# FFN in-projections as seven Strassen block products, the running sum z in DRAM, one new SBUF layout

## The chip, the cores and the metric

The kernel runs on one core of a Trainium2 chip. TensorE (PE) multiplies, VectorE (DVE), ScalarE (ACT) and GpSimd (POOL) do the elementwise work, SyncE (SP) issues most of the loads. The metric is the device time of one execution in microseconds, the median of several runs.

## The reference, cut to what matters

Two layers act on 512 latent and 256 context tokens of width 1024. Each layer is: half-step SwiGLU FFN, token mixer (chunked gMLP in layer 0, grouped-query attention in layer 1), half-step FFN; each sub-layer is modulated and closed by a LayerNorm of `ALPHA * x + sublayer`.

```python
def swiglu(h, w_in, w_out):
    g, u = jnp.split(h @ w_in, 2, axis=-1)          # w_in: 1024 x 2*2816
    return (jax.nn.silu(g) * u) @ w_out             # w_out: 2816 x 1024

def ffn_sublayer(x, shift, scale, gate, w_in, w_out, ln_g, ln_b):
    y = swiglu(modulate(x, shift, scale), w_in, w_out)
    return layer_norm(ALPHA * x + 0.5 * gate * y, ln_g, ln_b)
```

Three of the four FFNs see all 768 tokens (`plan` in `body`: layer 0 first and second FFN, layer 1 first FFN), the last one only the 512 latents. All matrix products are taken in three float32r passes (`split` makes `hi + lo`; the products are hi·hi, hi·lo and lo·hi).

## The kernel before, in words

The 2816 columns of g and of u are cut into 22 tiles of 128. For one tile, `in_proj` runs over 8 slices of K = 1024 and three passes with the weights stationary: 48 matmuls with 512 latent columns for g and u, then 48 with 256 context columns. ACT and DVE then make `silu(g) * u` and split it (`glu`, in `ffn`). After a chunk of 3 or 4 tiles (`FFN_CHUNKS`) `out_proj` multiplies it back: per block of 128 tokens and half of D, `accumulate` runs 3 matmuls of 512 columns for each tile of the chunk, DVE multiplies PSUM by the gate (L421) and adds the result to `z`, which stays in SBUF (L422).

Weights come through `load_raw` (SP, 512 KB each) and `pump`: ACT copies the high part of a 128x1024 tile (L134), DVE subtracts for the low part (L135). Six such tiles are in flight (`W_BUFS`).

Behind this run the fillers. `mod_unit` works out one modulation vector on DVE by 8 steps of two slices of `w_mod` (L247: one operation for each slice and condition), and reduces it over the partitions on POOL (L255); `affine` turns z into `ALPHA * (zhat * g + b)` on DVE (L395). `fill` issues one step; `FFN_FILLS` and `MOD_PLAN` say where.

The last chunk of a sub-layer is closed by `End.inner`: while the next block is on PE, a block's LayerNorm is taken, z is normalised in place, transposed on PE, and becomes h^T of the next sub-layer. `opening` runs the first two tiles of the next FFN on the latents while h^T of the context (blocks 4 and 5, `make_h`) is still being made.

PE and the start keep the order of the program (`Pinned`). The order on the other queues is fixed when the program is compiled, by a scheduler that takes ready instructions in program order; a tile is given out again once its last reader is done. All helpers' instructions are recorded under the helper's line (all matmuls: L67; all splits: L134 and L135).

Of the kernel before, what the change touches and what calls it, by code (L numbers as in the profile page):

```python
# [7 lines left out]
F32 = mybir.dt.float32  # L8
# [34 lines left out]
FFN_FILLS = [(4, 3), (4, 4), (0, 8), (0, 0)]  # L43
# [13 lines left out]
class Pinned:  # L57
    """An engine whose instructions keep the order of the program."""
# [13 lines left out]
class Backbone:  # L72
# [32 lines left out]
    def banks(self, paired):  # L105
        if paired and self.pairs:
            ps = self.pair()
            return [ps[:, 0:512], ps[:, 512:1024]]
        return [self.bank(), self.bank()]

    def t3(self, *shape):
        return self.main.tile([P, *shape], F32, tag="t3", bufs=5, name="t3")

    def mid(self, *shape):
        return self.main.tile([P, *shape], F32R, tag="mid", bufs=4, name="mid")

    def sm(self, shape, name, bufs=4, dt=F32):
        if shape == [P]:
            name, bufs = "s512", 6
# [4 lines left out]
    # ------------------------------------------------------------ primitives  # L124
    def mm(self, out, lhsT, rhs, start, stop):
        self.pe.matmul(out, lhsT, rhs, start=start, stop=stop)
# [5 lines left out]
    def split(self, hi, lo, src):  # L132
        """src = hi + lo, each of them exact in float32r"""
# [14 lines left out]
    # -------------------------------------------------------------- weights  # L148
    def weight_order(self):
        io = self.io  # L150
        seq = []

        def ffn(l, s):
            wi = io["ffn_w_in"][l, s].rearrange("(k p) f -> p k f", p=P)
            wo = io["ffn_w_out"][l, s]
            f0 = 0
            for n in FFN_CHUNKS:
                for f in range(f0, f0 + n):
                    for o in (0, D_FF):
                        seq.append(wi[:, :, o + f * P : o + f * P + P])  # L160
                for f in range(f0, f0 + n):
                    seq.append(wo[f * P : f * P + P, :])
                f0 += n

        ffn(0, 0)
        wi = io["gmlp_w_in"][0].rearrange("(k p) f -> p k f", p=P)
        for cc in range(GMLP_HALF // 512):
            for q in range(4):
                o = GMLP_HALF + cc * 512
                seq.append(wi[:, 2 * q : 2 * q + 2, o : o + 512])  # L170
        seq.append(wi[:, :, 0:P])
        j0 = 0
        for n in GMLP_CHUNKS:
            for j in range(j0 + 1, min(j0 + n + 1, GMLP_CH)):
                seq.append(wi[:, :, j * P : j * P + P])
            for j in range(j0, j0 + n):
                seq.append(io["gmlp_w_out"][0][j * P : j * P + P, :])
# [3 lines left out]
        wq = io["attn_w_qkv"][0].rearrange("(k p) f -> p k f", p=P)  # L181
        for o in (1024, 0, 512):
            for q in range(4):
                seq.append(wq[:, 2 * q : 2 * q + 2, o : o + 512])
        for h in range(N_HEADS):
            seq.append(io["attn_w_o"][0][h * P : h * P + P, :])
        ffn(1, 1)
        self.wseq, self.wraw, self.wready, self.wlive, self.reserve = seq, [], [], 0, 0

    def load_raw(self, most=RAW_BUFS):  # L190
        while len(self.wraw) < most and self.wseq:
            src = self.wseq.pop(0)
            raw = self.main.tile([P, 1024], F32, tag="raw", bufs=RAW_BUFS, name="raw")
            dst = raw if len(src.shape) == 2 else raw[:, :].rearrange("p (a b) -> p a b", b=src.shape[2])
            self.sp.dma_start(dst, src)
            self.wraw.append(raw)

    def pump(self, most=9):
        """split as many of the coming weights as there is room for"""
        self.load_raw()  # L200
        while self.wlive + self.reserve < W_BUFS and self.wraw and most:
            raw = self.wraw.pop(0)
            w = self.main.tile([P, 2, 1024], F32R, tag="w", bufs=W_BUFS, name="w")
            for c in self.cuts:
                self.split(w[:, 0, c], w[:, 1, c], raw[:, c])
            self.wready.append(w)
            self.wlive += 1
            self.load_raw()
# [12 lines left out]
    # ----------------------------------------------------------- modulation  # L221
    def mod_raw(self):
        """the next slice of w_mod: 128 rows by 512 columns"""
        while len(self.mraw) < MRAW_BUFS and self.mseq:
            l, i, half, k = self.mseq.pop(0)
            o = i * D + half * 512
# [1131 lines left out]
```

## Time and profile before

| | |
|---|---|
| median of 3 runs | 2980.02 us (2976.21 to 2981.7) |
| span of the profiled execution, first to last instruction | 2969.7 us |
| median less span | 10.3 us |
| busy in that span: PE, DVE, ACT, POOL | 2912.1, 1967.8, 928.6, 285.3 us |
| moved by DMA | 296.63 MB, mean 100 GB/s |

The page gives no total of the profiled execution beside its span; 10.3 us is what lies around it if it ran like the median. Groups of instructions are named by line, engine, operation, and out<-in by the program's names, with count, busy time and mean length. In a timeline a row begins with start and length in us, and may merge several instructions (x2).

### The profile page before, as it was taken

Reading aid. Unit: us, or ns where it says so; the run is one execution under the profiler, and the core shown is the slowest. Engines: PE = TensorE matmul, PEld = TensorE weight load, DVE = VectorE, ACT = ScalarE, POOL = GpSimd, SP = SyncE. Lnnn points to the kernel's source line nnn. Section 1 sums busy time; section 2 is a strip of 40 time slices with the busy share of each in tenths; the row PEclk is TensorE's granted clock in tenths of the full one; section 3 lists DMA queues with packets and bytes.
Section 4 is the critical chain, followed back from the end, with each engine's and each line's share of the span. In section 5 each row is a group of like instructions: output and inputs, shape, how many; then the busy total and the mean of one; then the engine's idle time right before and its main releaser. Section 6 shows DMA issues by size and latency. Waiting matters only on the chain.

```text
span 2969.7 us, 38390 instructions
## 1 busy us (share of the span) xinstructions
PE 2912.1 (98%) x15241; PEld 2493.9 (84%) x15241; DVE 1967.8 (66%) x3259; ACT 928.6 (31%) x1603; POOL 285.3 (10%) x180
## 2 busy tenths in 40 slices
PE   7999999999999999999999999999999989999998
PEld 5888888888888888878888888888888878888886
DVE  7867756574377778896866649854433687874455
ACT  6121221432342433512121134111122547722222
POOL 0201110011100000010111102000000022010001
PEclk9999999999999999999999999999999999999999
DMA  8434433144322322243333213532222140153232
GB/s 261 129 93 122 134 92 95 43 149 152 125 84 72 102 76 79 63 137 100 121 107 112 88 57 114 168 95 64 62 66 71 43 125 21 60 163 101 86 94 69
DMA packets 311178, 296.63 MB, mean 100 GB/s; under 512 B 12040, under 2 KB 248632, under 8 KB 311000
## 3 DMA queue, kind: packets, MB, share of 16 engines
q1 hardware_dynamic: 308120, 284.76, 31.8%
q0 software_dynamic: 2880, 9.44, 0.8%
q8 instruction: 119, 1.95, 0.3%
q14 instruction: 59, 0.48, 0.0%
HBM read 282.62 MB, written 11.53 MB: 99 GB/s over the span
## 4 chain that ended last, share of the span: by engine, by line
PE 85%; DVE 8%; ACT 2%; DMA 2%; issue 1%; POOL 1%; SPq 0%; DVEq 0%; POOLq 0%; ACTq 0%
PE ps L67 85%; DVE z L395 2%; DVE acc L247 2%; DVE w L135 1%; DMA mod_raw<-in_w_mod_dram 1%; PE pp L67 1%; DMA mraw<-in_w_mod_dram 0%; DVE z L67 0%; DVE mid L135 0%; POOL rs L145 0%; ACT t L867 0%; ACT t L865 0%; DVE t L538 0%; DVE t L421 0%; ACT pT L134 0%
## 5 line engine op out<-in xcount | busy, mean ns | idle before, releaser
L67 PE MATMUL ps<-hA,w 128*128 128x512 f32 (+1 forms) x4896 | 1110.1, 386 | 1.1 <-DVE w L135 0.9
L67 PEld LDWEIGHTS ps<-hA,w 128*128 128x128 f32 x4896 | 900.7, 188 | 180.8 <-DVE w L135 1.3
L67 PE MATMUL ps<-w,mid 128*128 128x512 f32 x3768 | 871.0, 391 | 8.6 <-ACT mid L134 5.2
L67 PEld LDWEIGHTS ps<-w,mid 128*128 128x128 f32 x3768 | 706.4, 189 | 157.9 <-ACT mid L134 6.8
L134 ACT CAST w<-raw 128x1024 fp32r<-128x1024 f32 (+1 forms) x363 | 368.7, 1032 | 894.1 <-issue 416.8
L135 DVE TENSOR_TENSOR w<-raw,w 128x1024 fp32r<-128x1024 f32 (+1 forms) x363 | 456.5, 1261 | 262.5 <-ACT w L134 261.8
L67 PEld LDWEIGHTS ps<-hB,w 128*128 128x128 f32 x3744 | 461.1, 192 | 8.8 <-DVE hB L135 1.0
L67 PE MATMUL ps<-hB,w 128*128 128x256 f32 x3744 | 464.2, 283 | 1.3 <-ACT hB L134 0.7
L421 DVE SCALAR_TENSOR_TENSOR t<-ps,gate 128x512 f32<-128x512 f32 x368 | 252.4, 689 | 196.0 <-PE ps L67 193.4
L538 DVE TENSOR_TENSOR t<-t,ps 128x512 f32<-128x512 f32 (+1 forms) x154 | 87.8, 571 | 349.2 <-PE ps L67 306.6
L134 ACT CAST mid<-t 128x512 fp32r<-128x512 f32 (+2 forms) x226 | 122.1, 556 | 553.3 <-DVE t L538 389.4
L247 DVE SCALAR_TENSOR_TENSOR acc<-mraw,cs,acc 128x512 f32<-128x512 f32 x392 | 277.8, 746 | 11.9 <-DMA mraw<-in_w_mod_dram 11.5
L422 DVE TENSOR_TENSOR z<-z,t 128x512 f32<-128x512 f32 x368 | 263.6, 723 | 8.7
L255 POOL PARTITION_ALL_REDUCE t<-acc x36 | 125.2, 3519 | 859.2 <-DVE z L422 570.7
L67 PE MATMUL ps<-w,hA 128*128 128x512 f32 x816 | 190.6, 390 | 0.0
L537 ACT ACTIVATE t<-ps 128x512 f32<-128x512 f32 (+1 forms) x154 | 77.9, 506 | 355.9 <-PE ps L67 324.8
L67 PEld LDWEIGHTS ps<-w,hA 128*128 128x128 f32 x816 | 153.3, 188 | 31.9
L145 POOL TENSOR_TENSOR rs<-ve,mhalf 128x1 f32<-128x1 f32 (+3 forms) x47 | 35.4, 756 | 1413.5 <-DVE ve L142 1057.5
L135 DVE TENSOR_TENSOR mid<-t,mid 128x512 fp32r<-128x512 f32 (+2 forms) x226 | 141.1, 637 | 44.9 <-ACT mid L134 44.7
L255 POOL PARTITION_ALL_REDUCE gate<-acc x20 | 75.2, 3791 | 247.9 <-DVE acc L247 240.5
L67 PE MATMUL ps<-w,hB 128*128 128x512 f32 x336 | 82.6, 397 | 2.8 <-ACT hB L360 2.1
L395 DVE SCALAR_TENSOR_TENSOR z<-ln_row,z 128x512 f32<-128x512 f32 x104 | 80.4, 820 | 1.9 <-DMA ln_row<-in_ln_b_dram 1.9
(151 smaller groups left out, 1570.9 us busy)
## 6 DMA issues: line engine op xcount, KB each, us to landing
raw<-in_ffn_w_in_dram SPq DMA_DIRECT2D x176, 512.0 KB
mraw<-in_w_mod_dram SPq DMA_DIRECT2D x256, 256.0 KB
raw<-in_ffn_w_out_dram SPq DMA_DIRECT2D x88, 512.0 KB
raw<-in_gmlp_w_in_dram SPq DMA_DIRECT2D x48, 512.0 KB
raw<-in_gmlp_w_out_dram SPq DMA_DIRECT2D x24, 512.0 KB
v_spill<-t POOLq DMA_DIRECT2D x36, 256.0 KB, 3.0
t<-v_spill SPq DMA_DIRECT2D x24, 384.0 KB
mod_raw<-in_w_mod_dram SPq DMA_DIRECT2D x16, 512.0 KB
```

Of the source, the lines that this page charges most:

```text
L67: return self.tc.keep_in_program_order(f(*args, **kwargs))
L134: i = self.act.copy(hi, src)
L135: self.dve.tensor_tensor(lo, src, hi.bitcast(F32), ALU.subtract)
L145: self.last_rstd = self.nc.gpsimd.tensor_tensor(rs, ve, self.mhalf[:, 0:1].to_broadcast([P, n]), ALU.pow).ins
L247: dve.scalar_tensor_tensor(accs[c], raw, cs, accs[c] if k else self.brow, ALU.mult, ALU.add)
L255: nc.gpsimd.partition_all_reduce(out, accs[c], P, bass_isa.ReduceOp.add)
L395: self.dve.scalar_tensor_tensor(z, row[:, s], ALPHA, z, ALU.mult, op)
L421: self.dve.scalar_tensor_tensor(tmp, banks[half], factor, self.gate[:, c, s], ALU.mult, ALU.mult)
L422: self.dve.tensor_tensor(self.z[b][:, s], self.z[b][:, s], tmp, ALU.add)
L537: self.act.activation(s[:, cols], g, AF.Silu)
L538: self.dve.tensor_tensor(s[:, cols], s[:, cols], u, ALU.mult)
```

## The change

**In-projections.** K is cut into two halves, the 768 tokens into two halves of 384 (`HT`), and [g u] is taken as two column blocks. A tile becomes seven products (Strassen's scheme in Winograd's form) instead of eight, each of 4 slices of K, three passes and 384 columns: 12 matmuls, 84 a tile. The products need seven combinations of h^T (`comb`: B11, B21, T1 to T4, B22, made by `combine`) and seven of the weights (`units`). The results are put together on DVE (`tile_strassen`).

**Weights** now come in units of 128x512, ten in flight (`W_BUFS`), raws of 256 KB, six in flight.

**z** is no longer kept in SBUF. Each half of a block of an out-projection goes to DRAM by an accumulating DMA on the POOL queue (`add_to_z`); so does `ALPHA` times the residual, from zhat stored in DRAM (`residual_unit`, a filler now). `End.begin` loads z back for the last chunk, which is still added in SBUF (`close`).

**Opening.** Four tiles are opened with their B11 and B21 products, while h^T of blocks 3 to 5 and the combinations are made. At the kernel's start only blocks 0 to 2 are made by quarters.

**SBUF** has nine boxes of 128x3072 for h^T, activations, z and the mixers' tiles, and six `q` tiles of 128x512; the last FFN (`ffn_latent`) and the mixers keep plain products. Chunks are now [4, 4, 2, 4, 4, 4] in an FFN and six of 4 (eight before) in gMLP; gates are kept in DRAM and loaded by `load_gate`; modulation vectors are planned in other sub-layers.

```diff
-FFN_CHUNKS = [4, 3, 3, 4, 4, 4]
-GMLP_CHUNKS = [3, 3, 3, 3, 3, 3, 2, 4]
-W_BUFS = 6
-RAW_BUFS = 3
-MRAW_BUFS = 3
+FFN_CHUNKS = [4, 4, 2, 4, 4, 4]
+GMLP_CHUNKS = [4, 4, 4, 4, 4, 4]
+W_BUFS = 10
+RAW_BUFS = 6
+MRAW_BUFS = 2
+OPEN = 4
+HALF = 3
 MOD_PLAN = [
-    [(0, 2), (0, 3), (0, 4), (0, 6), (0, 7)],
-    [(0, 5)],
-    [(0, 8), (1, 0), (1, 1), (1, 3), (1, 4)],
-    [(1, 2), (1, 6), (1, 7)],
-    [(1, 5)],
+    [(0, 2), (0, 3), (0, 4)],
+    [(0, 5), (0, 6), (0, 7), (0, 8)],
+    [(1, 0), (1, 1), (1, 2)],
+    [(1, 3), (1, 4), (1, 5), (1, 6)],
+    [(1, 7)],
     [(1, 8)],
 ]
...
+    def units(self, jobs):
+        dve = self.dve
+        for kind, srcs in jobs:
...
+            g1 = self.take()
+            if kind == "s":
+                yield self.unit_of(g1)
+            u1, u2 = self.take(), self.take()
+            s1, s2 = self.sums(), self.sums()
+            dve.tensor_tensor(s1, u1, u2, ALU.add)
+            dve.tensor_tensor(s2, s1, g1, ALU.subtract)
+            yield self.unit_of(s2)
...
+    def add_to_z(self, b, half, src):
+        s = slice(half * 512, half * 512 + 512)
+        op = ALU.add if (b, half) in self.z_begun else ALU.bypass
+        self.z_begun.add((b, half))
+        self.nc.gpsimd.dma_start(self.zsum[b][:, s], src, accum_op=op)
...
+    def combine(self, b, banks):
...
+        h1, h2 = self.q(512), self.q(512)
+        self.h_affine(b, 0, banks[0], False, h1)
+        self.h_affine(b, 1, banks[1], True, h2)
...
+        t1, t2, t4 = cut(self.spare()), cut(self.spare()), cut(self.q(512))
+        f32 = lambda name, x: part(name, x).bitcast(F32)
+        dve.tensor_tensor(t1, h1, f32("B11", 0), ALU.subtract)
+        dve.tensor_tensor(t1, t1, f32("B11", 1), ALU.subtract)
+        dve.tensor_tensor(t2, h2, t1, ALU.subtract)
+        put("T2", t2)
+        dve.tensor_tensor(h1, h2, h1, ALU.subtract)
+        put("T3", h1)
+        put("T1", t1)
+        dve.tensor_tensor(t4, f32("B21", 0), t2, ALU.subtract)
+        dve.tensor_tensor(t4, t4, f32("B21", 1), ALU.add)
+        put("T4", t4)
+        put("B22", h2)
...
+    def accumulate(self, b, half, acts, ws, factor):
+        ps = self.bank()
+        self.products(ps, b, acts, ws)
+        self.add_to_z(b, half, self.gated(b, half, ps, factor))
...
+    def product(self, ps, name, go_on=False):
+        (w,) = self.weights(1)
...
+        self.release(1)
+        self.pump(2)
...
+    def opening(self):
+        self.new_pieces()
+        for _ in range(OPEN):
+            t = self.open_first()
+            self.hook()
+            self.begun.append(self.open_second(*t))
...
+    def tile_strassen(self, m, opened):
...
+        self.product(b2, "T2")
+        dve.tensor_tensor(v, v, b2, ALU.add)
+        self.product(b4, "T3")
+        w = self.q(512)[:, 0:HT]
+        dve.tensor_tensor(w, v, b4, ALU.add)
+        self.product(b3, "T1")
+        dve.tensor_tensor(w, w, b3, ALU.add)
+        if opened is None:
+            self.product(b1, "B21", True)
+            g = self.q(512)[:, 0:HT]
+            act.activation(g, b1, AF.Silu)
+        self.product(b4, "T4", True)
+        c = self.q(512)[:, 0:HT]
+        dve.tensor_tensor(c, v, b4, ALU.add)
+        dve.tensor_tensor(g, g, c, ALU.mult)
+        self.split(m[:, 0, T1], m[:, 1, T1], g)
+        self.product(b3, "B22", True)
+        dve.tensor_tensor(v, v, b3, ALU.add)
+        act.activation(v, v, AF.Silu)
+        dve.tensor_tensor(v, v, w, ALU.mult)
+        self.split(m[:, 0, T2], m[:, 1, T2], v)
...
+            for f, m in enumerate(self.acts_places(size, TOK)):
+                self.tile_strassen(m, self.begun.pop(0) if self.begun else None)
+                if not (last and f == size - 1):
+                    self.fill(2)
+                acts.append(self.act_of(m))
+            if ci == 0:
+                self.load_gate(l, i + 2, nblocks)
             self.out_proj(acts, 0.5, nblocks, end if last else None)
```

More of the change, by code (lines that the diff above doesn't have):

```diff
@@ L287, in behind, with fill @@
+    def fill(self, n=1):
+        for _ in range(n):
+            todo, self.pending = self.pending, []
+            with self.behind():
+                for f in todo:
+                    f()
+                next(self.filler, None)
     @contextmanager
@@ new lines, in opening_latent, with part @@
+    def opening_latent(self):
+        ws = [self.weights(4) for _ in range(2)]
+        banks = [[self.bank(), self.bank()] for _ in range(2)]
+        early, late = slice(0, 2 * P), slice(2 * P, LAT)
+        def part(n, cols):
+            for x in range(2):
+                self.in_proj(banks[n][x][:, cols], ws[n][2 * x : 2 * x + 2], cols)
+        part(0, early)
+        self.hook()
+        part(1, early)
+        part(0, late)
+        yield banks[0]
+        self.release(4)
+        self.pump()
+        part(1, late)
+        yield banks[1]
+        self.release(4)
+        self.pump()
@@ L1127, in latent @@
             for x, ps in enumerate(banks):
[L1128 removed]
+                for b in range(HALF):
                     k = 2 * q + x
```

1082 lines of the change are left out of this document (565 added, 517 removed).

## The prediction

> **What bounds the kernel now.** I read the page's busy times and chain first, then the timeline of a quiet stretch of the second FFN, then the windows around its start.
>
> ```profile
> span 2969.7 us, 38390 instructions
> PE 2912.1 (98%) x15241; PEld 2493.9 (84%) x15241; DVE 1967.8 (66%) x3259; ACT 928.6 (31%) x1603; POOL 285.3 (10%) x180
> ...
> PE 85%; DVE 8%; ACT 2%; DMA 2%; issue 1%; POOL 1%; SPq 0%; DVEq 0%; POOLq 0%; ACTq 0%
> ```
>
> PE sets the end: of 2969.7 us it is without work for 57.6 (2969.7 - 2912.1). Only fewer matmul columns can gain much. DVE has a third of the span free as an average; where it lies decides.
>
> ```profile
> 1418.56 11.04 PE L67 MATMUL ps<-hA,w 128*128 128x512 f32 x48
> 1429.44 5.92 PE L67 MATMUL ps<-hB,w 128*128 128x256 f32 x48
> 1435.19 11.07 PE L67 MATMUL ps<-hA,w 128*128 128x512 f32 x48
> ```
>
> One tile of the in-projection takes 1435.19 - 1418.56 = 16.63 us. A 512-column matmul steps by (1429.44 - 1418.56)/48 = 226.7 ns, a 256-column one by (1435.19 - 1429.44)/48 = 119.8 ns.
>
> ```profile
> 1247.00:1313.50 66.50, 61.12 (x362) 53.91 (x360) 63.02 (x86) 18.72 (x30) 13.79 (x4) 0.99 0.43 131
> 1313.50:1770.00 456.50, 455.78 (x2405) 394.38 (x2405) 300.15 (x524) 89.59 (x128) 56.71 (x17) 0.99 0.34 102
> 1808.00:1868.00 60.00, 60.00 (x357) 53.32 (x354) 59.51 (x82) 14.69 (x26) 15.60 (x4) 1.00 0.44 133
> ```
>
> Columns: window, length, then busy PE, PEld, DVE, ACT, POOL. In the first chunk of an FFN DVE is already full (63.02 of 66.50, 59.51 of 60.00); PE idles 5.4 us there in the second FFN and none in the third. Behind that DVE is at 66% (300.15 of 456.50).
>
> **PE's part.** 384 columns are not in the trace. Halfway between the two steps is 173.2 ns; the ends are 170.0 (the 512-column price per column) and 179.7 (the 256-column price). A tile becomes 84 x 173.2 = 14.55 us, seven products of 2.08: 2.08 us less, or 1.54 to 2.35 by the ends. For 66 tiles that is 137 us (101 to 155). Out-projections and gMLP keep their columns (512 + 256 becomes 2 x 384 there).
>
> **DVE's part** pays for it. What one operation costs when DVE is full:
>
> ```profile
> 1421.88 1.21 DVE L135 TENSOR_TENSOR w<-raw,w 128x1024 fp32r<-128x1024 f32 x1
> 1423.01 0.68 DVE L422 TENSOR_TENSOR z<-z,t 128x512 f32<-128x512 f32 x1
> 1423.61 1.21 DVE L135 TENSOR_TENSOR w<-raw,w 128x1024 fp32r<-128x1024 f32 x1
> ...
> 1275.81 0.41 DVE L538 TENSOR_TENSOR t<-t,ps 128x256 f32<-128x256 f32 x1
> 1276.14 1.22 DVE L135 TENSOR_TENSOR w<-raw,w 128x1024 fp32r<-128x1024 f32 x1
> ...
> 1278.94 2.73 DVE L247 SCALAR_TENSOR_TENSOR acc<-mraw,cs,acc 128x512 f32<-128x512 f32 x4
> ...
> 1402.44 0.69 DVE L421 SCALAR_TENSOR_TENSOR t<-ps,gate 128x512 f32<-128x512 f32 x1 [0.62 <-PE ps L67]
> 1403.17 0.69 DVE L422 TENSOR_TENSOR z<-z,t 128x512 f32<-128x512 f32 x1
> ```
>
> Starts are 0.60 us apart for 512 elements (1423.01 to 1423.61), 1.13 for 1024, 0.33 for 256, hence 0.465 for 384; 0.67 for a step of the modulation; 0.13 more where an operation needs the one before (0.73). Before, a tile cost 2 x 1.13 + 2 x (0.60 + 0.33) = 4.1 us of DVE. After: seven splits and four sums of weights, nine operations of 384: 11 x 0.60 + 9 x 0.465 + 0.4 for dependence = 11.2 us, under 14.55 of PE.
>
> Fillers come on top, two steps a tile: 2 x 2 x 0.67 = 2.7 us for the residual, 2 x 4 x 0.67 = 5.4 for the modulation. Its reductions also hold DVE up:
>
> ```profile
> 1267.12 6.88 POOL L255 PARTITION_ALL_REDUCE gate<-acc  x2 [25.13 <-DVE acc L247]
> 1267.57 5.99 DVE L395 SCALAR_TENSOR_TENSOR z<-ln_row,z 128x512 f32<-128x512 f32 x3
> ```
>
> Three operations took 5.99 instead of 2.0, so 2.0 us for each reduction, one in two steps: 7.4 us a pair of steps. A tile then asks 18.6 of DVE in 14.55 of PE. Weights run ten units ahead in program order, so they don't starve; what is late is the GLU of the chunk's last tile, and PE waits for it in the out-projection. DVE before that point in a chunk of four: 4 x 11.2 + 3 x 7.4 (the fourth pair lies under the out-projection) + 4 more unit splits (2.4) - 4.5 (2.5 for blocks 3 to 5, needed later, and 2.0 that PE spends on the first three tiles) = 64.9, against 58.2: 6.7 us late. With residual steps: 50.8, nothing late. Out-projections (144 x 0.2267 = 32.6 us, DVE some 19) hide the rest, but their DVE time can't be used ahead, since ten units are all that may be ready. Two-condition modulation fills two such chunks in the second FFN, one in the third, some one and a half in the first: 13.4 + 6.7 + 10 us. The gMLP takes three vectors more: 7 steps x (4 x 0.67 + 1.0) + 8 splits + 6 statistics = 34.5 us of DVE for 32.6 of PE; 4 us in all (0 to 15).
>
> **Openings.**
>
> ```profile
> 1243.56 1.36 DVE L353 TENSOR_SCALAR t<-ps,modA,modB 128x128 f32<-128x128 f32 x4
> 1240.13 1.03 PE L67 MATMUL ps<-ident,z 128*128 128x128 f32 x8
> ```
>
> `combine` is 1.36 + 11 x 0.60 + 0.6 = 8.6 us of DVE a block, three blocks in order. PE needs T2 of block 5 after 8 x 2.08 + 3 x 1.03 = 19.7 us; DVE has it after the last LayerNorm (4.4), two blocks (17.2), the head of the third (4.0) and 10 splits and 3 sums (7.8) = 33.4. PE waits 13.7. To the end of chunk 0 DVE then has 4.6 + 26 splits and 14 sums (24.0) + four GLUs (18.4) + 8.1 - 4.5 = 50.6 against 20 x 2.08 = 41.6: 9.0 late. An opening loses 22.7.
>
> At the kernel's start:
>
> ```profile
> 0.00:68.40 68.40, 53.33 (x310) 37.70 (x310) 46.86 (x74) 43.38 (x57) 1.22 (x9) 0.98 0.90 272
> 111.84 33.13 PE L67 MATMUL ps<-w,mid 128*128 128x512 f32 x144
> ```
>
> The first out-projection begins at 111.84. Now DVE has 32 modulation splits (19.2), vectors and h^T (10), three combinations (25.8), 38 unit splits and 17 sums (33.0), GLUs (18.4), three modulation pairs (22.2), less 4.5 = 124, and idles about 15 us while loads land (21.5 of 68.4 before): 139, so +27 (+13 if only T2 is late).
>
> **Moves costed at nothing.** The accumulating DMA takes 0.6 us a half off DVE, off the path.
>
> ```profile
> 1447.09 0.62 ACT L134 CAST mid<-t 128x512 fp32r<-128x512 f32 x1 [5.64 <-DVE t L538]
> ...
> 672.28 2.15 POOL L654 DMA_DIRECT2D v_spill<-t  x4
> 673.08 1.21 DVE L135 TENSOR_TENSOR w<-raw,w 128x1024 fp32r<-128x1024 f32 x1
> ...
> DMA to landing us min/median/max: 2.3/3.0/5.0
> ```
>
> Four issues take 2.15 us of POOL and leave a split beside them at 1.21. Plain stores land in 3.0, at most 5.0; an accumulation also reads, so I take 3.0 to 10 (twice the slowest). Six `q` buffers at one per 2.72 us cover 16; behind two reductions in the POOL queue (6.88) still 9. If landing took 20, PE would stop for 20/6 - 2.72 = 0.6 us a half once the PSUM banks are full, 7 us an out-projection. Behind a waiting accumulation on POOL stand the reductions and, at a sub-layer's end, the LayerNorm's rstd, which comes five us after the last of them. Loading z back is 3.1 MB, 11.6 us at the start's 272 GB/s: the first box comes free with the last tile's B11 product, 12 us before PE needs it, the second is needed 16 us later; without that cover about 10 us each, six times. Behind a z load on SP stand weights, of which ten units are ready. ACT is busy 31% and gets seven copies and five evacuations a tile, at 0.62 or less under 8 of 14.55 us: nothing.
>
> [...]
>
> **Sum.** Columns in the 62 tiles behind the start's chunk: -129. Start +27. Openings of the second and third FFN 22.7 - 5.4 and 22.7: +40. Modulation chunks +30, gMLP +4. Together -28. The profiled execution spans 2969.7; 10.3 around it make the median, 2980. **Forecast 2952 us.** Own range 2915 to 2974 (the PE step's ends, and late chunks by half).
>
> **Rivals.** *Most of the gain stays*: GLUs and fillers slip under the out-projections, only T2 is late: -129 + 13 + 8 + 14 = -94, 2886 us. For it: DVE at 66% behind the opening. Against: fillers stand ahead of the next GLU in program order.
>
> *DVE becomes the bound; slower.*
>
> ```profile
> L538 DVE TENSOR_TENSOR t<-t,ps 128x512 f32<-128x512 f32 x88 | 60.4, 686 | 308.4 <-PE ps L67 306.6 <-ACT t L537 1.9
> L538 DVE TENSOR_TENSOR t<-t,ps 128x256 f32<-128x256 f32 x66 | 27.7, 419 | 40.7 <-ACT t L537 40.7
> L395 DVE SCALAR_TENSOR_TENSOR z<-ln_row,z 128x512 f32<-128x512 f32 x104 | 80.4, 820 | 1.9 <-DMA ln_row<-in_ln_b_dram 1.9
> ```
>
> If chains and waits keep DVE from packing, operations cost their full length: 0.69, 0.55 for 384, 0.75 and 0.82 for fillers. By the same counts a tile asks 11 x 0.69 + 9 x 0.55 = 12.5; a modulation chunk is 50.2 + 3 x 8.0 + 2.8 - 4.5 - 58.2 = 14.3 late (four and a half of them: 64); T2 comes at 36.3 and the rest of the opening at 57.6, so 16.6 + 16.0 = 32.6 (twice, less 5.4: 60); the start is 153, +41; gMLP +15, its upper end. -129 + 41 + 60 + 64 + 15 = +51, 3031 us. Between -28 and +51 it turns slower at a third of the way, when operations average 0.03 us over the packed step. For it: each tile's nine operations hang on PE one by one. Against: the full windows above ran packed.
>
> *The product isn't shorter*: if a matmul can't step faster than its weight load.
>
> ```profile
> L67 PEld LDWEIGHTS ps<-hB,w 128*128 128x128 f32 x3744 | 461.1, 192 | 8.8 <-DVE hB L135 1.0
> ```
>
> At 192 ns a tile takes 16.1, 33 us saved, fewer of the waits: about 2980. But 256-column matmuls step by 119.8 with the same load.
>
> **Chances.** Forecast 0.42, most of the gain 0.13, DVE-bound 0.35, no difference by either road 0.10. Range 2884 to 3034, from rival to rival. Six us (0.2%) is about what the runs can tell from no change. Faster 0.53, same 0.11, slower 0.36.
>
> **What would show it.** PE busy near 2775, the 84 matmuls of a tile in 14.5 us; DVE busy up to some 2250. Right, if PE waits for DVE (T2, then the GLU at the head of an out-projection) 14 and 9 us at each opening, 7 in modulation chunks, and hardly elsewhere. Wrong, if PE waits for weights (w) or `q` buffers through all tiles, for POOL or z loads at a sub-layer's end, or if starts on a full DVE are 0.69 apart.

## The result

The changed kernel takes 3157.22 us (median of four, 3152.75 to 3160.01) against 2980.18 (2976.21 to 2981.7): a ratio of 1.0596, with a 95% interval of 1.0581 to 1.0611. It is 177 us slower, where 28 us faster was forecast.

The page of the changed kernel: the span, the busy times, and the group of the products' matmuls (columns: count | busy us, mean ns of one | idle before them and its main releaser).

```profile
span 3156.9 us, 41429 instructions
PE 2846.4 (90%) x14449; PEld 2549.9 (81%) x14449; DVE 2269.3 (72%) x4179; ACT 1162.4 (37%) x2267; POOL 597.1 (19%) x593
...
L67 PE MATMUL ps<-comb,w 128*128 128x384 f32 x5544 | 1026.9, 345 | 153.9 <-DVE q L681 81.5
```

PE is busy 65.7 us less than before (2912.1 - 2846.4) and idle 310.5 us (3156.9 - 2846.4) instead of 57.6. So of the 137 us of columns that the products save, half doesn't show in PE's busy time, and 253 us of waiting came on top. Where it lies is read from windows, cut at the first matmul of each sub-layer. First the changed kernel, then the one before (columns: window, length, then busy PE, PEld, DVE, ACT, POOL; clock, DMA share, GB/s).

```profile
0.00:644.60 644.60, 557.96 (x2869) 507.69 (x2870) 483.26 (x880) 237.58 (x446) 116.63 (x122) 0.94 0.55 144
644.60:1358.50 713.90, 641.12 (x3225) 568.45 (x3224) 460.87 (x873) 250.95 (x500) 145.42 (x145) 0.95 0.56 147
1358.50:1936.70 578.20, 529.37 (x2689) 488.72 (x2688) 469.08 (x838) 200.93 (x372) 109.40 (x101) 0.96 0.55 139
1936.70:2504.40 567.70, 524.11 (x2697) 484.03 (x2696) 470.51 (x854) 201.45 (x377) 109.33 (x99) 0.97 0.59 150
2504.40:2771.60 267.20, 227.99 (x1285) 196.13 (x1284) 188.65 (x430) 156.86 (x382) 53.52 (x63) 0.94 0.33 97
2771.60:3156.90 385.30, 365.84 (x1691) 304.83 (x1689) 196.90 (x310) 114.64 (x193) 62.82 (x66) 0.98 0.59 153
```

```profile
0.00:596.10 596.10, 580.30 (x3133) 494.58 (x3134) 408.76 (x690) 167.72 (x251) 73.84 (x34) 1.00 0.40 121
596.10:1234.70 638.60, 635.34 (x3234) 542.31 (x3233) 441.01 (x745) 235.60 (x434) 38.63 (x47) 1.00 0.32 99
1234.70:1795.40 560.70, 554.60 (x2954) 480.04 (x2953) 395.10 (x669) 136.30 (x214) 73.24 (x26) 0.99 0.34 102
1795.40:2348.70 553.30, 552.24 (x2954) 478.33 (x2953) 316.58 (x473) 134.81 (x213) 33.14 (x14) 1.00 0.29 88
2348.70:2590.10 241.40, 225.65 (x1285) 194.77 (x1284) 192.10 (x404) 154.31 (x368) 40.83 (x44) 0.99 0.22 67
2590.10:2969.70 379.60, 364.00 (x1691) 303.83 (x1689) 214.28 (x283) 99.89 (x128) 25.66 (x15) 0.98 0.34 104
```

The differences add up to 187 us, that of the two spans, 10 more than the medians' 177. Every run of which both are recorded took 1.7 to 1.8 us longer than its span, so the profiled execution of the kernel before took about 2971.5 us, 9 under its median; the 10.3 us that were given as lying around its span are in the main this. The third column of numbers in this table is the prediction's terms, sorted by stage: the first FFN is +27 (start) - 18 x 2.08 + 10; the second 22.7 - 5.4 + 13.4 - 22 x 2.08; the third 22.7 + 6.7 - 45.8. The fourth is an experiment shown below, the new layout without the seven products.

| stage | before | after, difference | predicted | eight products, new layout |
|---|---|---|---|---|
| first FFN | 596.1 | 644.6, +48.5 | -0.4 | 630.5 |
| gMLP | 638.6 | 713.9, +75.3 | +4 | 710.8 |
| second FFN | 560.7 | 578.2, +17.5 | -15.1 | 558.6 |
| third FFN | 553.3 | 567.7, +14.4 | -16.4 | 558.4 |
| attention | 241.4 | 267.2, +25.8 | 0 | 269.6 |
| last FFN and end | 379.6 | 385.3, +5.7 | 0 | 385.2 |

More than half of the loss, 107 us, lies in three stages whose matmuls the products don't touch. The rest lies in the three FFNs, which lose 80 us instead of gaining 32.

What PE waits for in the changed kernel (columns: us in total, times, longest):

```profile
PE ps L67 <- DVE q L681: 81.5, 32, 7.3
PE ps L67 <- DVE s L130: 49.8, 1, 49.8
PE ps L67 <- ACT comb L534: 34.0, 3, 18.8
PE ps L67 <- DVE kT L130: 25.2, 4, 11.6
PE ps L67 <- ACT q L854: 20.7, 4, 11.0
...
PE ps L67 <- DVE q L683: 12.4, 9, 3.5
...
PE ps L67 <- ACT acts L129: 10.1, 7, 3.3
```

Three kinds of place stand out. `L681` and `L683` lie inside a Strassen tile: VectorE reads the banks of T3 and T1 there, and T4 and B22 are accumulated onto those banks, so PE must wait for the reads. `s L130` is one transposed spatial weight of the gMLP, and `q L854` an evacuation there; `kT L130` are the attention's K transposes. `comb L534` is the operand T2 at the openings. The wait for the last GLU at an out-projection (`acts`), which the prediction named, is 10 us in all (and 3.5 more at `acts L130`).

**The gMLP.** PE's timeline at the end of its in-projection, then VectorE's in the middle of it and at the moment that PE is released:

```profile
869.69 0.27 PE L67 MATMUL ps<-ident,s 128*128 128x128 f32 x1
919.79 0.58 PE L67 MATMUL ps<-s,ones 128*128 128x256 f32 x1 [49.83 <-DVE s L130]
```

```profile
738.53 0.69 DVE L372 SCALAR_TENSOR_TENSOR mraw<-acc,mraw 128x512 f32<-128x512 f32 x1 [4.85 <-DMA mraw<-zhat]
741.09 1.90 DVE L372 SCALAR_TENSOR_TENSOR mraw<-acc,mraw 128x512 f32<-128x512 f32 x3 [1.87 <-DMA mraw<-zhat]
...
748.55 0.69 DVE L372 SCALAR_TENSOR_TENSOR mraw<-acc,mraw 128x512 f32<-128x512 f32 x1 [4.35 <-DMA mraw<-zhat]
...
759.38 0.69 DVE L372 SCALAR_TENSOR_TENSOR mraw<-acc,mraw 128x512 f32<-128x512 f32 x1 [6.55 <-DMA mraw<-zhat]
...
916.48 2.46 DVE L855 BATCH_NORM_STATS2 vst<-q 128x6 f32<-128x512 f32 x4
918.86 0.67 DVE L130 TENSOR_TENSOR w<-raw,w 128x512 fp32r<-128x512 f32 x1
919.45 0.28 DVE L130 TENSOR_TENSOR s<-ps,s 128x128 fp32r<-128x128 f32 x1
```

PE finishes the in-projection at 869.7. VectorE gets to its last statistics at 916.5, because the steps of residual and modulation stand ahead of them in its queue. Those steps are not long in work: three residual operations take 1.90 us. They are long in waiting, 4 to 7 us for a load each pair, because a residual step holds one of only two buffers from its load to the landing of its store to z. Over this whole in-projection, up to 919.8, VectorE is idle 87 of 275 us: 61 for loads, 15 for the reductions on GpSimd, 10 for ScalarE. From 870 to 919.8 it is busy 39 of 50 us, working off what it is late.

**The clock.** PE's rows in three chunks of the second FFN, the last row undisturbed:

```profile
1605.16 7.05 PE L67 MATMUL ps<-comb,w 128*128 128x384 f32 x24 [3.44 <-DVE q L681]
...
1647.24 16.92 PE L67 MATMUL ps<-comb,w 128*128 128x384 f32 x84 [6.70 <-DVE q L681]
1665.72 14.86 PE L67 MATMUL ps<-comb,w 128*128 128x384 f32 x84 [1.56 <-DVE q L681]
...
1740.95 25.15 PE L67 MATMUL ps<-comb,w 128*128 128x384 f32 x144
```

Undisturbed, 144 matmuls take 25.15 us, 174.7 ns each with the last one's drain, so the prediction's 173.2 was right. After a wait of 1.56 us, 84 take 14.86, nearly the same. After 3.44 us 24 of them take 7.05 instead of some 4.4, and after 6.70 us 84 take 16.92. The granted clock in the profile is 0.59 of full speed over those 24, and 1.00 over the undisturbed 144. In the second and third FFN, behind their openings, a stall of over 3 us thus cost 1.6 to 2.7 us more (the least in the third, where 24 take 6.02 after 3.50 us and 84 take 16.43 after 7.27), in matmuls that ran slower behind it. Where it begins isn't sharp: at the opening of the second FFN 24 matmuls take 6.02 us, at a clock of 0.71, after a wait of only 1.78 us, and the same 24 take 4.45 after 1.77 us at the opening of the third. The timeline has 27 stalls of over 3 us (the first at 16 us, the last at 2821) and 4 in the kernel before: 23 more make 37 to 62 us by this estimate, at least half of the 71 us by which PE's busy time fell short of 137. Nearly all of the 71 lies in the products: their matmuls are busy 1026.9 us, where 66 tiles of 14.55 make 960.

### The profile page after: what moved, and what is told of

Its sections match the earlier page's. It is cut to its first block, busy times and chain, and to the rows that moved or that the text cites. A ratio compares the mean times of both kernels' runs of the same rounds, so it can differ in the third digit from the quotient of the medians.

```text
span 3156.9 us, 41429 instructions
## 1 busy us (share of the span) xinstructions
PE 2846.4 (90%) x14449; PEld 2549.9 (81%) x14449; DVE 2269.3 (72%) x4179; ACT 1162.4 (37%) x2267; POOL 597.1 (19%) x593
## 5 line engine op out<-in xcount | busy, mean ns | idle before, releaser
L67 PE MATMUL ps<-comb,w 128*128 128x384 f32 x5544 | 1026.9, 345 | 153.9 <-DVE q L681 81.5
L67 PEld LDWEIGHTS ps<-comb,w 128*128 128x128 f32 x5544 | 1000.9, 195 | 175.7 <-DVE q L681 62.7
L67 PE MATMUL ps<-w,acts 128*128 128x512 f32 x3768 | 873.1, 392 | 13.7 <-ACT acts L129 10.1
L67 PEld LDWEIGHTS ps<-w,acts 128*128 128x128 f32 x3768 | 707.5, 189 | 166.4 <-ACT acts L129 14.0
L129 ACT CAST w<-raw 128x512 fp32r<-128x512 f32 x678 | 415.1, 621 | 843.6 <-PE ps L67 580.3
L130 DVE TENSOR_TENSOR w<-raw,w 128x512 fp32r<-128x512 f32 x678 | 484.2, 722 | 185.4 <-ACT w L129 177.8
L381 POOL DMA_DIRECT2D zsum<-q x288 | 245.5, 891 | 1133.5 <-DVE q L575 1091.2
L67 PE MATMUL ps<-h,w 128*128 128x384 f32 (+2 forms) x2304 | 448.0, 354 | 0.9 <-DVE w L130 0.9
L67 PEld LDWEIGHTS ps<-h,w 128*128 128x128 f32 x2304 | 404.5, 189 | 38.4 <-DVE w L130 1.1
L67 PE MATMUL ps<-w,h 128*128 128x512 f32 x1200 | 280.1, 394 | 24.1 <-ACT q L854 20.7
L67 PEld LDWEIGHTS ps<-w,h 128*128 128x128 f32 x1200 | 226.7, 190 | 75.3 <-ACT q L854 23.0
L130 DVE TENSOR_TENSOR w<-sums,w 128x512 fp32r<-128x512 f32 x264 | 183.5, 706 | 47.5 <-ACT w L129 45.5
L372 DVE SCALAR_TENSOR_TENSOR mraw<-acc,mraw 128x512 f32<-128x512 f32 x104 | 71.3, 696 | 86.5 <-DMA mraw<-zhat 76.2
L130 DVE TENSOR_TENSOR acts<-q,acts 128x384 fp32r<-128x384 f32 (+1 forms) x133 | 76.5, 576 | 3.0 <-ACT acts L129 2.4
```

The lines of the kernel that those rows point to most:

```text
L67: return self.tc.keep_in_program_order(f(*args, **kwargs))
L129: i = self.act.copy(hi, src)
L130: self.dve.tensor_tensor(lo, src, hi.bitcast(F32), ALU.subtract)
L372: self.dve.scalar_tensor_tensor(raw, row, ALPHA, raw, ALU.mult, op)
L381: self.nc.gpsimd.dma_start(self.zsum[b][:, s], src, accum_op=op)
```

## Experiments

Each is a change of the changed kernel, 3157.22 us, and its ratio is to the kernel before. The first four ask which part is to blame, the others why.

**Fillers under the out-projections.**

```diff
-                if not (last and f == size - 1):
+                if (l, i + 2) not in self.mod_done:
                     self.fill(2)
...
-            self.out_proj(acts, 0.5, nblocks, end if last else None)
+            self.out_proj(acts, 0.5, nblocks, end if last else None, 1)
...
                     self.accumulate(b, half, acts, ws, factor)
                     self.pump(1)
+                    self.fill(fills)
```

> The Strassen FFNs issue their filler steps (residual and modulation) under the out-projections, one for each block and half, instead of two behind each tile; only the first FFN's first chunk keeps them, because its gate vector is due then. Theory (fillers put DVE behind PE, and in a tile PE has only the products T1 and B21, 4.2 us, before T4 goes onto the bank that DVE still has to read): PE's waits for L681 and L683, 94 us now, fall under 40 (the openings stay), PE is busy some 30 us less as well because its clock no longer drops behind the stalls, and the time falls from 3157 to 3070 to 3110. Rival 1 (DVE simply has more work than these stages have time): the wait moves into the out-projections, PE idle stays within 15 us of 310, 3140 to 3170. Rival 2 (a tile's own splits and sums are what is late): L681 stays above 70 us, 3140 or more.

Measured: 3271.69 us, 1.0986 (1.0961 to 1.1012). PE's waits (the code's line 682 is 681 above), and two of VectorE's:

```profile
PE ps L67 <- DVE q L682: 152.5, 16, 25.9
...
PE ps L67 <- DVE q L575: 34.0, 8, 10.4
```

```profile
DVE acc L323 <- DMA mraw<-in_w_mod_dram: 100.9, 95, 4.2
DVE mraw L372 <- DMA mraw<-zhat: 98.0, 32, 8.0
```

The second rival's bounds are met (over 70 us, 3140 or more), but no theory had this: the waits neither shrank nor stayed, they grew. Twelve steps now come in 33 us, one in 2.7, and their loads don't keep that pace: these two waits of VectorE were 73.8 and 76.2 us, those for the reductions on GpSimd went from 16 to 59. VectorE leaves an out-projection up to 26 us late, and PE meets that in the next tile. So it matters how densely the fillers stand, and not only beside what.

**The gMLP's first group early, and its fillers thinned.**

```diff
+        following = group(0)
+        next(following)
         for cc in range(CC):
...
-            if cc == CC - 1:
-                following = group(0)
-                next(following)
             self.token_proj(range(NB), evacuate)
-        next(following)
+            if cc == CC - 2:
+                next(following)
```

> In the gMLP the first group's spatial weight is loaded ahead of the in-projection and transposed behind its fifth part of six, as in the kernel before; nothing else. Theory (DVE runs some 50 us behind PE there, because filler steps stand in its queue and wait for their loads; the last statistics of v, at 918.9 us, are late as well): the 49.8 us wait only moves to the spatial mixing, behind the two products that PE can do meanwhile (18.9 us): 3135 to 3150, and a PE gap of 25 to 35 us ahead of the first mixing. Rival (the order of that one transpose is the cause): the gap disappears, 3100 to 3112.

The second kernel has this, and `token_proj(range(NB), evacuate, fills=1 if cc % 2 == 0 else 0)`.

> As e2_group_early, and the filler steps of the gMLP's in-projection are halved: one behind each weight in its parts 1, 3 and 5, none in parts 2, 4 and 6; the others follow one by one in the 24 mixing tiles as before. Theory (fillers make DVE late): the gMLP's in-projection ends without a wait over 10 us, the PE waits of 49.8 us (L130) and 20.7 us (L854) fall under 15 together, PE's clock there rises from 0.88 towards 1, and the time is 3075 to 3100. Rival (the fillers cost the same wherever they stand): the mixing tiles get longer by what the in-projection gains, 3125 or more.

Measured: 3161.11 us for the first (two runs), 3101.80 for the second, 1.0414 (1.0389 to 1.0438). In the first, the wait moved as the theory said, and to two places: an evacuation (16.58 us) and, behind the two products, the first mixing.

```profile
858.02 31.02 PE L67 MATMUL ps<-w,h 128*128 128x512 f32 x129 [16.58 <-ACT q L856]
...
889.00 16.83 PE L67 MATMUL ps<-h,w 128*128 128x384 f32 x96
927.65 0.58 PE L67 MATMUL ps<-s,vn 128*128 128x256 f32 x1 [21.83 <-ACT vn L129]
```

(The code's line 856 is 854 above.) The order of the transpose gained nothing, not even the 7 to 22 us that the theory gave it. With half the fillers in the in-projection (the others follow in the mixing, and the time is 2 us above its bracket) the whole stage takes 650.3 us instead of 713.9, at a clock of 0.99 instead of 0.95, though VectorE does the same work in it (465 us instead of 461) and waits as long for the fillers' loads (57.9 us instead of 54.1), only spread:

```profile
639.90:1290.20 650.30, 638.81 (x3226) 567.65 (x3225) 464.96 (x872) 247.87 (x500) 143.78 (x145) 0.99 0.61 162
```

**Eight products in the new layout**, first in two FFNs, then in all three.

```diff
-            (self.ffn, 0, 6, NB, "s"),
-            (self.ffn, 1, 0, NB, "s"),
+            (self.ffn_plain, 0, 6, NB, "p"),
+            (self.ffn_plain, 1, 0, NB, "p"),
...
+    def plain_half(self, m, ws, x):
+        cols = slice(x * HT, x * HT + HT)
+        pg, pu = self.part_bank(), self.part_bank()
+        self.in_proj(pg, ws[0:2], cols)
+        self.in_proj(pu, ws[2:4], cols)
```

> The second and third FFN make their in-projections with eight block products (96 matmuls of 384 columns a tile, four weight units, no sums) in the new layout, with the same fillers, accumulating DMAs and z in DRAM; the first FFN keeps the seven. The two FFNs took 1114 us before and 1146 after. PE has 44 x 2.08 = 92 us more to do in them. Theory (the seven products' DVE work and their bank reuse cost what they save, the layout costs these two stages little): the two FFNs take 1110 to 1135 us, 3120 to 3147 in all. Rival (the layout alone costs them: fillers waiting for their loads, accumulating DMAs): the two FFNs take 1160 to 1200, 3170 to 3210, and the seven products do gain by themselves.

> All three 768-token FFNs make their in-projections with eight block products in the new layout; modulation plan, fillers, buffers, accumulating DMAs and z in DRAM are those of the changed kernel. What it differs from the kernel before by is the layout with its fillers, what it differs from the changed kernel by is the seven products. Theory (both lose: gMLP and attention by fillers, the FFNs by the products' work on VectorE): the first FFN takes 596 to 610 us (596 before, 645 after), gMLP 705 to 725, the two later FFNs 1110 to 1125, attention 265 to 285, the last FFN 373, together 3075 to 3115. Rival (the first FFN loses by the layout, by z's stores and the residual's loads, not by the products): it takes 625 or more, 3115 and up.

Measured: 3131.88 us, 1.0511 (1.0491 to 1.0532), and 3116.07 us, 1.0465 (1.0448 to 1.0483). The first one's two FFNs:

```profile
1360.50:1917.70 557.20, 553.29 (x2954) 521.25 (x2953) 306.40 (x546) 149.19 (x275) 107.75 (x101) 1.00 0.57 140
1917.70:2477.00 559.30, 555.49 (x2962) 523.38 (x2961) 311.17 (x563) 149.31 (x280) 106.44 (x99) 0.99 0.58 147
```

They take 1116.5 us, 29 less than with seven products and 2.5 more than before, at full clock and with VectorE at 55%. So in these stages the layout, with z in DRAM and the accumulating DMAs, costs next to nothing, and the loss comes with the seven products. It takes both them and the modulation: with the seven and most of the modulation left out (below) the two FFNs take 1100.3 us, 16 less than with eight. Over the whole kernel the layout and its fillers cost 137 us (3116.07 against 2978.71) and the products 41 more (3157.22 - 3116.07). By stage the layout's part is the gMLP's 72 us, the attention's 28, and 34 in the first FFN, which the rival had right. With eight products in all three, the first FFN's first out-projection stands at:

```profile
133.00 32.94 PE L67 MATMUL ps<-w,acts 128*128 128x512 f32 x144
```

It comes at 133.0 us instead of 111.84, 21 of the 34. But this start also lacks the products that the changed kernel does between its loads, so this part isn't the layout's for certain.

**Banks of their own for T4 and B22.**

```diff
-        dve.tensor_tensor(w, v, b4, ALU.add)
+        dve.tensor_tensor(c, v, b4, ALU.add)
         self.product(b3, "T1")
-        dve.tensor_tensor(w, w, b3, ALU.add)
+        dve.tensor_tensor(w, c, b3, ALU.add)
+        dve.tensor_tensor(v, v, b3, ALU.add)
...
-        self.product(b4, "T4", True)
+        self.product(b5, "T4")
...
-        self.product(b3, "B22", True)
+        self.product(b6, "B22")
```

> Each tile's products T4 and B22 get PSUM banks of their own instead of going onto the banks of T3 and T1; VectorE then adds the T1 bank twice (one operation of 384 more a tile, 0.465 us, 31 us in all). Theory A (the reuse of the banks inside the tile is the cause: PE has 4.2 us of cover there, and now about a tile): the waits L681 and L683, 94 us, fall under 20, nothing takes their place but up to 25 us at the out-projections, PE's clock in the FFNs returns to 0.99, and the time is 3060 to 3110. Theory B (VectorE has more to do in a modulated chunk than PE gives it time for, and the reused bank is only where that shows first): the waits move to the last GLU ahead of the out-projections (acts) and to the next products, the two later FFNs stay within 15 us of 1146, and the time is 3140 to 3180.

Measured: 3153.61 us, 1.0577 (1.0554 to 1.0600). The waits inside the tiles are gone, and the out-projections have them:

```profile
PE ps L67 <- ACT acts L129: 81.5, 17, 10.8
```

81.5 us, to the digit what `L681` had, though 10 of it stood at `acts` already. The modulated chunk's four tiles take 66.2 us instead of 78.2, and the out-projection behind them 40.8 instead of 32.8. In all that is 107.0 us instead of 111.0, and the whole time lies in theory B's bracket. Theory B holds: the bank reuse is only the place where late work is met first.

**Less modulation in the second and third FFN.**

```diff
-            for k in range(KD):
+            for k in range(KD if self.n not in (2, 3) else 2):
```

> In the second and third FFN the modulation sums only the first two of their eight 128-row parts (six of eight loads and their VectorE operations are left out, so the later sub-layers get other numbers); residual steps, products and layout stay. Theory (the fillers' load on VectorE makes PE wait inside the tiles): of the two FFNs' waits on L681 and L683, 67 us, only the openings' 19 stay, and they take 1065 to 1095 us together instead of 1146: 3076 to 3106 in all. Rival (the tile's own chain of nine operations with the splits is too long for its cover): they take 1125 or more, 3136 and up.

Measured: 3116.34 us, 1.0462 (1.0441 to 1.0484); the two FFNs take 551.8 + 548.5 = 1100.3 us, 46 less, 5 above the bracket, and the whole time is 10 above its own. The kernel leaves out three quarters of the modulation's loads and sums, but not the reductions, and so the steps end early: the chunks of the second FFN that took 78.2 and 68.9 us have no filler left, and take 58.1 each, which is what PE needs. The second FFN's opening chunk stays at 90 us and the chunk behind it, with the last residual steps, at 60.8; the one of two tiles, into which six reductions now fall, grows from 35.3 to 38.6.

**The attention's first projection without fillers, and three buffers for their loads.**

```diff
-        self.token_proj(range(NB), kv_out, 1)
+        self.token_proj(range(NB), kv_out, 0)
```

> No filler steps in the attention's first token projection (K and V); they follow in the later ones. Theory (as in the gMLP, filler steps that wait for their loads hold VectorE's queue): PE's wait for the K transposes (L130, 25 us) falls under 8, the attention takes 245 to 252 us instead of 267, 3132 to 3145 in all. Rival (the wait comes from the K norms and rope themselves, or the fillers only move to the next stage): 3152 to 3160.

```diff
-RAW_BUFS = 6
-MRAW_BUFS = 2
+RAW_BUFS = 5
+MRAW_BUFS = 3
```

> Three buffers for the fillers' loads, as in the kernel before, instead of two, and five instead of six for the weights' (there is no room for one more). Theory (a residual step holds its buffer from its load through the sum to the landing of its accumulating DMA, so that two buffers make VectorE wait for loads: 150 us in L372 and L323): these waits fall under 100, the gMLP's 49.8 us wait of PE falls by 15 us or more, 3110 to 3145. Rival (VectorE's order and work decide, not the loads): waits of VectorE move to other lines, 3150 to 3165; and if five weight buffers are too few, PE waits for w and it gets slower.

Measured: 3160.44 and 3148.78 us (two runs each). In the first the rival holds: the attention takes 268.5 us instead of 267.2. PE's wait for the K transposes fell from 25.2 to 10.4 us, but waits behind it grew, PE's waits there fell only from 39 to 35 us in all, and its busy time rose from 228 to 234. In the second the loads are faster for the fillers and slower for the weights:

```profile
DVE sums L251 <- DMA raw<-in_ffn_w_in_dram: 85.4, 25, 7.5
DVE mraw L372 <- DMA mraw<-zhat: 40.6, 12, 6.7
DVE acc L323 <- DMA mraw<-in_w_mod_dram: 36.2, 32, 3.0
```

The last two were 76.2 and 73.8, the first 36.3. The gMLP takes 692.7 us (21 less), its wait 33.6 instead of 49.8; the first FFN takes 663.9 (19 more). So the two buffers are a part of the gMLP's loss, and the time missed its bracket by 4 us while the first FFN paid 19; that this is the price of the weights' lost buffer is read from the 85.4, and not tried apart.

**Modulation moved.** The first kernel has the thinned gMLP and the banks of their own as well.

```diff
 MOD_PLAN = [
     [(0, 2), (0, 3), (0, 4)],
-    [(0, 5), (0, 6), (0, 7), (0, 8)],
-    [(1, 0), (1, 1), (1, 2)],
-    [(1, 3), (1, 4), (1, 5), (1, 6)],
-    [(1, 7)],
+    [(0, 5), (0, 6), (0, 7), (0, 8), (1, 0), (1, 1)],
+    [(1, 2), (1, 3)],
+    [(1, 4), (1, 5), (1, 6), (1, 7)],
+    [],
     [(1, 8)],
```

> e3_gmlp_thin and e5_own_banks together, and modulation vectors moved to where VectorE has time: two more under the gMLP's mixing (five filler steps in three tiles instead of three), two instead of three in the second FFN, none of them and no residual step in its first chunk, in the third FFN one of two conditions and three of one instead of two and two, none in the attention. Theory (VectorE's load in the modulated chunks decides): FFN 2 takes 540 to 560 us instead of 578, FFN 3 545 to 562 instead of 568, attention 250 to 262 instead of 267, the mixing tiles stay at 9.8 us: 3035 to 3075. Rival (VectorE is full wherever its steps go): the mixing tiles get longer by the added steps and it stays at 3085 to 3110.

The second has the plan of the kernel before, and three steps a tile in two FFNs.

> The modulation plan of the kernel before in the changed kernel: two of three vectors that the gMLP makes ahead of the second FFN go back into the first FFN (five instead of three there), the gMLP keeps one of four, the second FFN makes five instead of three, the third three instead of four, the attention one as now. So that the steps find a place, the first two FFNs issue three filler steps a tile instead of two. Theory (VectorE has no room left in the FFNs, room in the gMLP only if its loads keep up): the gMLP takes 640 to 660 us instead of 714, the first FFN 665 to 700 instead of 645, the second 600 to 630 instead of 578, the third 555 to 568 instead of 568: 3110 to 3180. Rival (moving the vectors into the gMLP was the loss by itself): FFN 1 and 2 grow by less than 25 us together, 3060 to 3105.

Measured: 3086.85 us, 1.0362 (1.0347 to 1.0378), and 3237.78 us, 1.0875 (1.0852 to 1.0898). In the first the attention falls to 247.1 us and the third FFN to 559.1, as expected; the second FFN, at 566.2, misses its bracket, and the gMLP grows from 650.3 to 693.9 (tiles of 9.8 us become up to 11.2), so here the rival holds: its room was used up. The second FFN's opening chunk had no fillers in this kernel:

```profile
1360.26 0.69 PE L67 MATMUL ps<-comb,w 128*128 128x384 f32 x1 [7.96 <-ACT comb L534]
1361.41 43.56 PE L67 MATMUL ps<-comb,w 128*128 128x384 f32 x239 [0.47 <-DVE comb L535]
1404.81 0.39 PE L67 MATMUL ps<-w,acts 128*128 128x512 f32 x1
```

Behind T2 PE runs through. The chunk takes 75.5 us (1329.27 to 1404.81), 14.2 over PE's 61.3 (20 + 8 products and three blocks' transposes), where the changed kernel takes 89.4 (1358.5 to 1447.9).

In the second kernel the gMLP is back at 652.0 us, but the first two FFNs take 705.1 and 649.1, 131 us more, beyond what the theory gave them: they have no room at all.

**The reductions on TensorE.**

```diff
-                nc.gpsimd.partition_all_reduce(out, accs[c], P, bass_isa.ReduceOp.add)
...
+        for kk in range(4):
+            self.mm(ps[:, 4 * kk : 4 * kk + 4], acc[:, kk * P : kk * P + P], self.ones4, True, True)
```

> The 56 reductions over partitions that end the modulation sums go from GpSimd to TensorE: four matmuls with four columns of ones give the columns of a vector (40 times), one gives the row of a gate (16 times); VectorE's four products with the identity behind each go too. VectorE is held 2.0 us less and does 0.9 us less for each, some 120 to 160 us in all; TensorE gets 15 to 45 us more. Theory (VectorE's load sets the FFNs' and the gMLP's waits): VectorE's waits for GpSimd vanish, gMLP 690 to 705 instead of 714, FFN 2 and 3 take 5 to 20 us less each, 3100 to 3140. Rival (TensorE waits for the late sums in its own order, or the added matmuls cost what the waits gave): 3150 to 3200.

Measured: 3126.13 us, 1.0490 (1.0468 to 1.0511).

```profile
PE 2896.2 (93%) x14777; PEld 2578.9 (82%) x14777; DVE 2174.2 (70%) x3891; ACT 1180.7 (38%) x2323; POOL 405.4 (13%) x538
...
PE ps L67 <- DVE acc L323: 50.2, 5, 22.5
```

VectorE has 95 us less to do, PE 50 more, and the kernel is 31 us faster; gMLP 688.6, the second and third FFN 566.2 and 562.1. PE's wait for `s L130` falls from 49.8 to 5.7 us, and it now waits 50 us for the sums themselves. Both theories have a part: less load on VectorE pays even with PE's time as the price.

No version beats the kernel before. The best of each stage over all runs that do the whole work (630.5, 650.3, 557.2, 558.4, 247.1 and 385.2), which can't even be had together, adds up to 3028.7, against a span of 2969.7.

## Why the prediction was wrong

Two steps of it failed above all. It priced VectorE's fillers by their work, without their waits and their pace, and so put the gMLP and the attention at 4 us together where they lost 101, and the modulation chunks of the second and third FFN at 20 where they lost 68. And it let PE stall without a loss of clock. Term by term:

- **PE's columns.** Right in size: 174.7 ns with drain against 173.2. The step from there to 137 us of time failed, because PE's clock was taken as given. It fell behind the stalls (0.59 over 24 matmuls behind one of 3.44 us), and 71 us of the gain did not show in PE's busy time.
- **VectorE's packed starts.** Right: three operations in 1.90 us are 0.605 apart ((1.90 - 0.69) / 2), and its busy time is 2269.3 us where "up to some 2250" was given. The second rival had the right sign and the wrong mechanism: operations aren't longer, VectorE stands still between them (87 of 275 us in the gMLP's in-projection).
- **The openings.** T2's wait was given as 13.7 us, the rest of the chunk as 9.0. The opening without fillers lost 14.2, idle time and slow matmuls together. The rest measured 89.4 - 75.5 = 13.9, and it vanished with the chunk's fillers. That kernel also has banks of their own; with these alone and the fillers kept, the opening's products run through as well and PE waits 8.9 us behind them, for `acts`. So the fillers' part is between 9 and 13.9 us. The mechanism was right, the term (28.1 for 22.7) a fifth too small.
- **Modulation chunks.** "6.7 us late" each was the wrong size. The four chunks behind the opening of the second FFN that have modulation steps are 4.4, 6.2, 20.0 and 10.7 us late (62.6, 35.3, 78.2 and 68.9 us for four, two, four and four tiles of 14.55), 41 where 13.4 was given; in the third FFN it is 27 for 6.7. The step that failed is the credit: the prediction's own load, 18.6 us of VectorE in 14.55 of PE, makes 16.2 us a chunk of four, and it took off the fourth pair of steps, which was to lie under the out-projection, and 4.5 us, which left 6.7. The three chunks of four tiles that are full of two-condition steps lost 20.0, 10.7 and, in the third FFN, 19.6 us, 16.8 on the average. That the credit alone is to blame is not shown. The place was wrong too, inside the tiles and not at the out-projection, but the experiment with banks of their own shows that the place makes little difference (107.0 us against 111.0). The sum let VectorE work without a pause and PE stall without a loss of clock. VectorE's waits in the second FFN behind its first chunk:

```profile
DVE q L575 <- PE ps L67: 36.8, 23, 2.0
DVE sums L251 <- DMA raw<-in_ffn_w_in_dram: 17.5, 6, 5.2
DVE w L130 <- ACT w L129: 13.3, 18, 1.5
```

  Beside PE's out-projections it waits for weight loads and for ScalarE's halves of the splits. That the loads are late because VectorE itself frees their buffers late is argued, not shown.
- **The start.** The first out-projection begins at 154.8 us against 111.84, +43 where +27 was given; T2 alone kept PE waiting 18.8 (`comb L534`).
- **The gMLP, "4 us in all (0 to 15)".** The largest failure, 71 us of 215. VectorE's work was not counted too low (34.5 us for each of six parts of 32.6; it was busy 188 in all, 31.3 a part). Its waiting, the 87 us above, was not counted, and a late VectorE was taken to cost only the difference. Thinning the steps gave back 64 us with the same work and as much waiting for loads, where VectorE had the room to catch up before PE needed it.
- **"Moves costed at nothing."** Right for what the text followed: no wait for `q` buffers above 7 us in all, none for z's loads, and the eight-product FFNs in the new layout take what they took. Wrong for the fillers' two buffers, which the text didn't mention: a third gave the gMLP 21 us. Gates loaded from DRAM, not mentioned either, kept VectorE 19.1 us at the head of out-projections.
- **The attention, not in the prediction.** +25.8 us. Without a modulation vector in it the loss shrinks to 5.7, though the kernel before works out one there as well; that its mechanism is the gMLP's, steps that wait for loads at the head of VectorE's queue, is argued from VectorE's 18 us of such waits between 2504 and 2612, and not shown apart.

The chances put 0.35 on a VectorE that bounds, and the range ended at 3034 since no case in it gave the gMLP more than 15 us, or the attention and the last FFN anything.

What stays open: how the first FFN's 48.5 us divide between layout and products at its start, and the last FFN's 5.7 us.

## What to carry to other kernels

A step that ran "in the background" on VectorE cost its wait as well as its work here (4 to 7 us of wait for a load beside 1.90 us of work in three steps): price such a step by its load, its buffer's whole round trip and the pace at which it is issued, in every stage that issues it, including those that the change seems to leave alone. When work is taken from the busiest engine and put on another, look at the chunks in which that other engine is already full, and not at its average; here its lateness turned up at the dependence that came first, and with that one removed at another (81.5 us of PE's waiting at `L681`, then 81.5 at `acts`, which had 10 before). And count stalls of TensorE by number as well as by length: the matmuls behind one of over 3 us took 1.6 to 2.7 us longer here.

## What the runs showed of the hardware

An accumulating DMA took GpSimd longer to issue here than a plain one, 0.85 to 0.89 us against 0.54. The first store to a half block is plain, the later ones add. The residual's stores in the gMLP, all of them first ones, take 0.54 us each, as do the plain stores of v in the same kernel (0.54); those of the second FFN that add take 0.85 to 0.89 us (from 1480 us on), and the out-projections' stores, most of which add, 891 ns in the mean. How much later they land is not clear: 5.0 us in the median, against 4.6 for the plain stores of v beside them, which had landed in 3.0 in the kernel before.

```profile
L381 POOL DMA_DIRECT2D zsum<-q x288 | 245.5, 891 | 1133.5 <-DVE q L575 1091.2
...
zsum<-q POOLq DMA_DIRECT2D x288, 256.0 KB, 5.0
```

The loss of clock behind a stall was not foreseen: 294 ns a matmul over the 24 behind a stall of 3.44 us, and no loss to speak of, 177 ns over 84, behind one of 1.56 us. Near 1.8 us both were seen, 6.02 us for 24 behind 1.78 and 4.45 behind 1.77.
